# A rarely taken branch's body in the straight line and announced early, and accumulator banks opened with f16 instead of f32 zeros

## The chip, the core and the metric

The kernel runs on one core of one Trainium2 chip. The core has five instruction streams: TensorE (PE; its weight loads are listed apart as PEld), VectorE (DVE), ScalarE (ACT), GpSimd (POOL) and SyncE (SP, which only issues DMAs). The metric is the device time of one execution in microseconds (us), as the median of several executions. A "q" behind an engine's name in a row (PEldq) means the engine's sequencer: waits, branches and issues, during which the engine itself may still work through what was queued.

## What is computed

One decoder layer on 256 tokens of width 2048, all in float32 at the interface. The change touches the second of its three parts, a retrieval of single-neuron experts (PEER). Of 128 x 128 = 16384 experts each token picks 16 in each of 8 heads:

```
eidx, gates = top16 of (key scores a + key scores b), softmax      # per token and head
act  = gelu(u[eidx] . x)                                           # one number per pick
out  = sum over picks of gates * act * v[eidx]                     # 2048 wide
x    = LN2(alpha * x + out)
```

In front of it stand two kinds of attention with LN1; behind it `x = LN3(alpha*x + sigmoid(x W_g) * (p W_p))`.

## The kernel before

The first 88 tokens are treated sparsely: POOL gathers the rows of u and v that they picked (tile `gb`), and DVE multiplies and adds them. The other 168 tokens (`NDT`) are treated densely on TensorE, in two phases:

- The **u phase** multiplies all 128 groups of 128 experts by the 168 tokens, one f32 product of 128 x 128 by 128 x 168 per sixteenth of the width (tile `ps_u`), and ACT takes the gelu (L1114). DVE, ACT and small f16 products (`ps_G`) turn that into a weight per expert and token, which goes to memory (`s_w`), and into a list of the experts that any of these tokens picked.
- The **v phase** walks that list in blocks of 128 experts. For each block POOL gathers two tiles, `vf` (128 rows of v, 1 MB) and `wc` (their weights, 128 x 168); TensorE multiplies each of the 16 column blocks of `vf` by `wc` and adds into six banks of PSUM, `psv` (`v_mm`, L1209). Five buffers of `vf` (`WF`) and eight of `wc` turn around; a gather waits until TensorE has released its buffer.

The list's length is known only at run time. A fixed number of blocks is always done (46 and 40, `CAPS`); 42 further blocks (`rest`) are done only if the list is longer. That is the branch of L1334: `more` is a count that DVE makes, every engine loads it into a register (L1252) and compares it with zero. On TensorE the body of the branch is 672 products. On these inputs the list fits, so the body is jumped over. The instructions of one engine lie in memory in one order: first the code ahead of the compare, then the arms of the branch in an order that `preferred_fallthrough_block` sets, then the code behind. The false arm holds the bookkeeping of the skipped work: on TensorE one wait for its own earlier products with an addition to its counter, on POOL four waits and one addition.

The last three of the always done blocks (`held`) are multiplied behind the branch, bank by bank, so that DVE can add each finished bank to the residual (`v_out`, L1224) while TensorE goes on; then follow transposes (`res2`, L1278 and L1280, with the sparse part's products L915 and L917), LN2, and the gate product `ps_gate` (L217 to L219), whose weights `ple_gate` SP loads and ACT and DVE split in two (L119, L120).

Before the first `v_mm`, each of the six banks is opened by a product of zeros (`v_bank`, L1216), so that all later products can add: the stationary operand is the f32 identity, the moving one a column of zeros read 504 times (three groups of 168; 168 times for the last bank). The first four banks are those that the u phase used, so an opening waits until ACT has taken the gelu out of that bank.

The order of each engine's instructions is made by a scheduler with a simulated timeline; `keep` pins an instruction to the order in which it is written.

Of the kernel before, what the change touches and what calls it, by code (L numbers as in the profile page):

```python
# [9 lines left out]
F32 = mybir.dt.float32  # L10
F32R = mybir.dt.float32r
F16 = mybir.dt.float16
# [7 lines left out]
P = 128  # L20
# [45 lines left out]
STAG, LEAD, NWC = 3, 4, 8  # L66
# [92 lines left out]
def build(tc, a, out):  # L159
    nc = tc.nc  # L160
# [6 lines left out]
    def pbank(pool, name, tag="bank", bufs=4):  # L167
        return pool.tile([P, 512], F32, name=name, tag=tag, bufs=bufs)
# [3 lines left out]
    ident = c0p.tile([P, P], F32, name="ident")  # L172
# [446 lines left out]
    gin = pools.open("gin", "left", bufs=1)  # L619
    io128 = gin.tile([P, P], F16, name="io128")  # L620

    zero = gin.tile([P, 1], F32, name="zero")
    nc.gpsimd.memset(zero, 0.0)
    eig, eact, ew = [], [], []
    for i, (_, n) in enumerate(GROUPS):
# [55 lines left out]
    keep = tc.keep_in_program_order  # L681
# [131 lines left out]
    def gathers(n):  # L813

        nonlocal due
        due += n
        while due >= 1:
            due -= 1
            run(sparse, 1)
# [283 lines left out]
    def run(work, n):  # L1103

        for _ in range(n):
            if next(work, "end") == "end":
                return True
        return False
# [63 lines left out]
    rest = [(i, b) for i, (_, n) in enumerate(PARTS) for b in range(CAPS[i], n)]  # L1172

    def v_fetch(i, b, vpool, wpool, tags):

        vf = vpool.tile([P, D], F32, name="vf", tag=tags[0], bufs=WF if vpool is sup else 1)
        wc = wpool.tile([P, NDT], F32, name="wc", tag=tags[1], bufs=NWC if vpool is sup else 1)
        for dst, src, idx in ((wc, a[f"s_w{i}"].rearrange("p a t -> (p a) t"), idxW[i]),
                              (vf, a["v_rows"], idxV[i])):
            keep(nc.gpsimd.indirect_dma_start(  # L1180
                out=dst, out_offset=None, in_=src,
                in_offset=bass.IndirectOffsetOnAxis(ap=idx[:, b:b + 1], axis=0)))
        return vf, wc
# [24 lines left out]
    def v_mm(d, vf, wc, last):  # L1208
        return nc.tensor.matmul(psv[d // 3][:, d % 3 * NDT:(d % 3 + 1) * NDT],  # L1209
                                vf[:, d * P:(d + 1) * P], wc, start=False,  # L1210
                                stop=last and (d % 3 == 2 or d == ND - 1))

    def v_bank(pool, n):

        ps = pbank(pool, "ps_v")
        keep(nc.tensor.matmul(ps[:, :n], ident, zero.to_broadcast([P, n]),  # L1216
                              start=True, stop=False))
        return ps

# [8 lines left out]
    def v_blocks(n, wpool, between=lambda: None):  # L1228

        for _ in range(n):  # L1230
            while order and len(fetched) <= LEAD and (not order[0][0] or len(idxV) > 1):
                fetched.append(v_fetch(*order.pop(0), sup, wpool, ("wf", "wc")))
            block = fetched.pop(0)
            for d in range(ND):
                v_mm(d, *block, False)
                if d % 8 == 7:
                    between()

    marked = False
    psv = [v_bank(pp, 3 * NDT) for _ in range(4)] + [v_bank(pa, n * NDT) for n in (3, 1)]  # L1240
    done = False

# [5 lines left out]
    for b in range(CAPS[0]):  # L1248
        if b == CAPS[0] - LEAD:
            while not done:  # L1250
                done = run(work, 1)
            more = nc.values_load(total[0:1, 0:1], min_val=0, max_val=NIA * NKEY)  # L1252
# [70 lines left out]
    N1 = CAPS[1]  # L1323
    for b in range(LEAD + 1, N1 - STAG):
        v_blocks(1, wcq)
        gathers(GV)
        if b == N1 - STAG - 1:
            while not run(sparse, 1):
                pass
# [1 line left out]
    natural_parts(ylp)  # L1331

    fbp = pools.open("fbp", "left", bufs=1)
    with tc.If(more > 0, preferred_fallthrough_block=False):  # L1334
        for i, b in rest:
            block = v_fetch(i, b, fbp, fbp, ("vf", "wc_"))
            for d in range(ND):
                v_mm(d, *block, False)
# [57 lines left out]
    def ln2_T(t, d0, nd):  # L1396
        ps = pbank(pp, "ps_x2T")
        for j in range(nd):
            keep(nc.tensor.transpose(ps[:, j * P:(j + 1) * P],  # L1399
                                     x2[t][:, (d0 + j) * P:(d0 + j + 1) * P], ident))  # L1400
        return ps[:, :nd * P].rearrange("p (j n) -> p j n", j=nd)
# [101 lines left out]
    ps = ln2_T(0, 0, 2)  # L1503
# [17 lines left out]
    ps = ln2_T(1, 0, 4)  # L1521
# [8 lines left out]
    ps = ln2_T(1, 4, 4)  # L1530
# [8 lines left out]
    ps = ln2_T(0, 8, 4)  # L1539
# [7 lines left out]
    ps = ln2_T(0, 12, 4)  # L1547
# [4 lines left out]
    for d0, k0, k1 in ((8, 12, 14), (12, 14, 16)):  # L1552
        ps = ln2_T(1, d0, 4)
# [157 lines left out]
```

## Time and profile before

| | us |
|---|---|
| median of 3 timed runs | 1710.34 (1708.72 to 1712.31) |
| the profiled execution, its own time | 1708.22 |
| its span, first to last instruction | 1706.4 |
| TensorE busy | 1682.3 (99% of the span) |
| weight loads busy | 1563.7 (92%) |
| VectorE, ScalarE, GpSimd busy | 1098.9, 556.1, 609.5 |
| mean granted TensorE clock | 0.997 of full speed |

The profile lists, for every group of instructions, how long the engine was busy in it and how long it stood idle before it, with what ended the idle time; "issue" means that nothing which the profile shows was waited for. TensorE's f32 products appear twice, as two records of weight load and product each. A record's duration (306 ns for 128 x 168) is longer than the distance from one start to the next (142 ns), because products overlap in the array; the distance is what a product costs.

### The profile page before, as it was taken

How to read it: one execution, taken by the hardware profiler on the slowest of the kernel's cores; microseconds unless marked ns; L12 is line 12 of the kernel's file. 1: busy time of each engine (PE TensorE's matmuls, PEld its weight loads, DVE VectorE, ACT ScalarE, POOL GpSimd, SP SyncE). 2: the span in 40 equal slices, each digit the busy share in tenths (PEclk: the TensorE clock that was granted, in tenths of full speed). 3: DMA queues.
4: the chain of work that ended last, by engine and by line, in shares of the span. 5: the costliest groups of instructions: out<-in, count | busy, mean ns of one | idle time of the engine just before them, and what ended most of it. 6: DMA issues, size and time to landing. Idle time of an engine off the chain costs nothing. (4 is left out here: it accounts for less than half of the span.)

```text
span 1706.4 us, 29275 instructions
## 1 busy us (share of the span) xinstructions
PE 1682.3 (99%) x11258; PEld 1563.7 (92%) x11258; DVE 1098.9 (64%) x2290; ACT 556.1 (33%) x1396; POOL 609.5 (36%) x624
## 2 busy tenths in 40 slices
PE   9999999999999999999999999999999999998998
PEld 7888888888889999999999999999999999998886
DVE  5565489763589779844467765785776943333676
ACT  5677468753111100010044552005553000001452
POOL 0134023103345422722232322137554787673000
PEclk9999999999999999999999999999999999999999
DMA  7544644483998999999999999979999999997571
GB/s 294 195 155 162 234 160 156 156 323 133 338 419 327 390 421 417 419 420 421 421 415 405 371 384 392 422 293 394 392 383 382 418 412 415 401 396 281 187 269 50
DMA packets 97444, 555.63 MB, mean 326 GB/s; under 512 B 13366, under 2 KB 16966, under 8 KB 41846
## 3 DMA queue, kind: packets, MB, share of 16 engines
q0 software_dynamic: 43056, 285.38, 41.7%
q1 hardware_dynamic: 52086, 264.99, 40.3%
q10 hardware_dynamic: 2160, 3.34, 0.6%
q8 instruction: 92, 1.51, 0.3%
q14 instruction: 50, 0.41, 0.1%
HBM read 536.80 MB, written 17.04 MB: 325 GB/s over the span
## 5 line engine op out<-in xcount | busy, mean ns | idle before, releaser
L210 PE MATMUL ps_u<-XF,wf 128*128 128x168 f32 x3936 | 581.3, 308 | 7.5 <-DMA wf<-peer_u 7.1
L210 PEld LDWEIGHTS ps_u<-XF,wf 128*128 128x128 f32 x3936 | 562.5, 190 | 14.1 <-issue 11.8
L1209 PE MATMUL ps_v<-wc,vf 128*128 128x168 f32 x2752 | 414.8, 309 | 5.5 <-issue 5.5
L1209 PEld LDWEIGHTS ps_v<-wc,vf 128*128 128x128 f32 x2752 | 395.9, 191 | 7.3 <-issue 6.8
L120 DVE TENSOR_TENSOR wl<-wf,wh 128x1024 fp32r<-128x1024 f32 (+1 forms) x199 | 212.7, 1092 | 109.8 <-ACT wh L119 108.2
L854 DVE SCALAR_TENSOR_TENSOR gb<-gb,xq 128x2048 f32<-128x2048 f32 x88 | 203.4, 2316 | 99.0 <-DMA gb<-u_rows,eig 99.0
L864 DVE SCALAR_TENSOR_TENSOR y<-gb,ew,y 128x2048 f32<-128x2048 f32 x78 | 183.0, 2346 | 76.4 <-DMA gb<-v_rows,eig 76.3
L119 ACT CAST wh<-wf 128x1024 fp32r<-128x1024 f32 (+1 forms) x199 | 172.0, 892 | 121.0 <-PE ps_v L219 33.0
L1114 ACT ACTIVATE A<-ps_u 128x168 f32<-128x168 f32 x128 | 39.6, 310 | 459.7 <-PE ps_u L210 456.8
L198 PE MATMUL ps_qk<-X,wh 128*128 128x512 f32 x512 | 185.2, 401 | 0.0
L886 POOL DMA_INDIRECT gb<-u_rows,eig x88 | 94.6, 1075 | 246.6 <-DVE gb L854 151.4
L886 POOL DMA_INDIRECT gb<-v_rows,eig x88 | 104.3, 1185 | 132.6 <-DVE y L864 36.4
L200 PE MATMUL ps_qk<-X,wl 128*128 128x256 f32 x512 | 145.7, 285 | 0.0
L943 ACT ACTIVATE hi<-eq,ghf 128x68 f16<-128x68 f16 (+1 forms) x336 | 113.0, 336 | 87.4 <-DVE eq L937 87.3
L1180 POOL DMA_INDIRECT vf<-v_rows,idxV x86 | 107.2, 1246 | 83.9 <-PE ps_G L958 45.1
L1180 POOL DMA_INDIRECT wc<-s_w,idxW x86 | 102.9, 1197 | 40.4 <-issue 24.9
L198 PEld LDWEIGHTS ps_qk<-X,wh 128*128 128x128 f32 x512 | 96.4, 188 | 21.9 <-issue 1.0
L210 PE MATMUL ps_q<-XF,wf 128*128 128x256 f32 x512 | 113.5, 379 | 0.0
L944 ACT ACTIVATE lo<-eq,glf 128x68 f16<-128x68 f16 (+1 forms) x336 | 112.3, 334 | 0.0
L968 DVE SCALAR_TENSOR_TENSOR A<-ps_G,A 128x18 f32<-128x18 f32 (+2 forms) x168 | 46.9, 308 | 100.4 <-PE ps_G L958 44.0
L210 PEld LDWEIGHTS ps_q<-XF,wf 128*128 128x128 f32 x512 | 95.9, 190 | 12.3
L200 PEld LDWEIGHTS ps_qk<-X,wl 128*128 128x128 f32 x512 | 96.3, 188 | 2.5 <-issue 1.3
(309 smaller groups left out, 2127.2 us busy)
## 6 DMA issues: line engine op xcount, KB each, us to landing
wf<-peer_u SPq DMA_DIRECT2D x123, 1024.0 KB
wf<-w_qk SPq DMA_DIRECT2D x64, 512.0 KB
wf<-w_out SPq DMA_DIRECT2D x32, 512.0 KB
wf<-peer_wq SPq DMA_DIRECT2D x16, 1024.0 KB
wf<-ple_gate SPq DMA_DIRECT2D x16, 1024.0 KB
s_w<-A SPq DMA_DIRECT2D x14, 672.0 KB
wf<-w_v SPq DMA_DIRECT2D x16, 512.0 KB
wf<-w_sv SPq DMA_DIRECT2D x15, 512.0 KB
```

Of the source, the lines that this page charges most:

```text
L119: self.order(nc.scalar.copy(wh, src))
L120: self.order(nc.vector.tensor_tensor(wl, src, wh.bitcast(F32), op=ALU.subtract))
L198: nc.tensor.matmul(ps, wh[:, j * P:(j + 1) * P], xt[:, dt, :], start=dt == 0, stop=False)
L200: nc.tensor.matmul(ps[:, :T], wl[:, j * P:(j + 1) * P], xt[:, dt, :T], start=False, stop=dt == ND - 1)
L210: nc.tensor.matmul(ps[:, :T - t0], wf[:, dt * P:(dt + 1) * P], xt[:, dt, t0:], start=dt == 0, stop=dt == ND - 1)
L854: keep(nc.vector.scalar_tensor_tensor(g, g, 1.0, xq[i], op0=ALU.mult, op1=ALU.mult, accum_out=eact[i][:, j:j + 1]))
L864: keep(nc.vector.scalar_tensor_tensor(ys[i], g, ew[i][:, j:j + 1], ys[i], op0=ALU.mult, op1=ALU.add))
L886: keep(nc.gpsimd.indirect_dma_start(out=g, out_offset=None, in_=a[kind], in_offset=bass.IndirectOffsetOnAxis(ap=eig[i][:, 0, j:j + 1], axi ...
L943: nc.scalar.mul(hi[:, j, :], eq[:, j, :], ghf[:, t])
L944: nc.scalar.mul(lo[:, j, :], eq[:, j, :], glf[:, t])
L1180: keep(nc.gpsimd.indirect_dma_start(out=dst, out_offset=None, in_=src, in_offset=bass.IndirectOffsetOnAxis(ap=idx[:, b:b + 1], axis=0)))
L1209: return nc.tensor.matmul(psv[d // 3][:, d % 3 * NDT:(d % 3 + 1) * NDT], vf[:, d * P:(d + 1) * P], wc, start=False, stop=last and (d % 3 = ...
```

## The change

Three edits, none of which changes a result. The `zero` column is f16 instead of f32, and the openings use `io128` (an f16 table of 0 to 127, there since the top-k stage) as stationary operand in place of the f32 identity: zero times anything finite is zero. The branch is told to lay its true arm, the body, next behind the compare, where the false arm was. And a place is marked in the loop over v's blocks, one block ahead of the branch in the source, for a hint to TensorE alone that this branch is likely taken.

```
-    zero = gin.tile([P, 1], F32, name="zero")
+    zero = gin.tile([P, 1], F16, name="zero")
...
-        keep(nc.tensor.matmul(ps[:, :n], ident, zero.to_broadcast([P, n]),
+        keep(nc.tensor.matmul(ps[:, :n], io128, zero.to_broadcast([P, n]),
                               start=True, stop=False))
...
     for b in range(LEAD + 1, N1 - STAG):
         v_blocks(1, wcq)
         gathers(GV)
+        if b == N1 - STAG - 2:
+
+            tc.mark_branch_hint_location("rest", "LikelyTaken", [mybir.EngineType.PE])
...
-    with tc.If(more > 0, preferred_fallthrough_block=False):
+    with tc.If(more > 0, preferred_fallthrough_block=True, label="rest"):
```

In the built programs the streams of DVE, ACT and SP hold the same instructions in the same order; POOL's differs only in the order of the branch's two arms. On TensorE three places differ.

First, the openings at the start of the v phase (`ps_u` is the u phase's bank, `ps_v` a bank of v, `io_4038` is io128). Before:

```order
L210 MATMUL ps_u<-XF,wf 128x168 x52
L1216 MATMUL ps_v<-zero,ident 128x504 x3
L1209 MATMUL ps_v<-wc,vf 128x168 x7
L1216 MATMUL ps_v<-zero,ident 128x504 x2
L1216 MATMUL ps_v<-zero,ident 128x168
L1209 MATMUL ps_v<-wc,vf 128x168 x9
```

And in the change:

```order
L210 MATMUL ps_u<-XF,wf 128x168 x52
L1216 LDWEIGHTS io_4038
L1216 MATMUL ps_v<-zero,io_4038 128x504
L1216 LDWEIGHTS io_4038
L1216 MATMUL ps_v<-zero,io_4038 128x504
L1216 LDWEIGHTS io_4038
L1216 MATMUL ps_v<-zero,io_4038 128x504
L1209 MATMUL ps_v<-wc,vf 128x168 x9
L1216 LDWEIGHTS io_4038
L1216 MATMUL ps_v<-zero,io_4038 128x504
```

Two more openings and 7 products follow. The openings of banks 4 to 6 moved from behind 7 products to behind 9, and each is one weight load and one product where an f32 product runs as two of both.

Second, the branch on TensorE, before (672 products are 42 blocks; the second 672 is the body, the first the blocks ahead of the branch; TENSOR_LOAD reads the count):

```order
L1209 MATMUL ps_v<-wc,vf 128x168 x672
L1252 TENSOR_LOAD total
L1334 COMPARE_AND_BRANCH
L1334 UNCONDITIONAL_BRANCH
L1209 MATMUL ps_v<-wc,vf 128x168 x672
L1334 UNCONDITIONAL_BRANCH
L1209 MATMUL ps_v<-wc,vf 128x168 x18
```

And in the change:

```order
L1209 MATMUL ps_v<-wc,vf 128x168 x672
L1252 TENSOR_LOAD total
L1337 COMPARE_AND_BRANCH
L1209 MATMUL ps_v<-wc,vf 128x168 x672
L1337 UNCONDITIONAL_BRANCH x2
L1209 MATMUL ps_v<-wc,vf 128x168 x18
```

Before, the false arm lies directly behind the compare and ends in the branch that jumps over the body; now the compare itself jumps over the body, to a false arm that lies directly ahead of the code behind the branch, so that this arm's own closing branch leads to the next instruction.

Third, the hint. TensorE's stream in the change begins:

```order
L1704 UNCONDITIONAL_BRANCH
L1704 BRANCH_PREFETCH_HINT
L319 MATMUL ps_zero<-M 128x256 x3
L217 MATMUL ps_v<-wh,X 128x512 x2
L218 MATMUL ps_v<-wl,X 128x512 x2
```

The hint waits for nothing, nothing pins it, and the scheduler has put it at the very beginning of the program, some 1560 us of work ahead of the branch; it stands nowhere else.

## Rows read from the trace of the kernel before

**Rows 1.** The page: busy time of the engines and their share.
```profile
PE 1682.3 (99%) x11258; PEld 1563.7 (92%) x11258; DVE 1098.9 (64%) x2290; ACT 556.1 (33%) x1396; POOL 609.5 (36%) x624
```

**Rows 2.** Waits of TensorE from 1150 us on: total us, times, longest.
```profile
PE ps_v L1209 <- issue: 5.5, 2, 5.4
PE ps_x2T L1399 <- ACT x L1417: 0.5, 1, 0.5
PE ps_fin L1601 <- ACT diag L1598: 0.5, 1, 0.5
```

**Rows 3.** TensorE's timeline at the openings: start, length, merged records.
```profile
1155.51 2.88 PE L1216 MATMUL ps_v<-zero,ident 128*128 128x504 f32 x6
1158.23 2.16 PE L1209 MATMUL ps_v<-wc,vf 128*128 128x168 f32 x14
1160.22 2.15 PE L1216 MATMUL ps_v<-zero,ident 128*128 128x504 f32 x6
1162.21 2.73 PE L1209 MATMUL ps_v<-wc,vf 128*128 128x168 f32 x18
1164.77 0.19 PE L951 MATMUL ps_G<-hi,ohb 128*128 128x60 f16 x1
1164.80 0.19 PE L952 MATMUL ps_G<-lo,ohb 128*128 128x60 f16 x1
```

**Rows 4.** Weight loads and ScalarE at the openings, from their timelines.
```profile
1157.27 0.30 PEld L1216 LDWEIGHTS ps_v<-zero,ident 128*128 128x128 f32 x2 [0.72 <-ACT A L1114]
1156.93 0.48 ACT L1114 ACTIVATE A<-ps_u 128x168 f32<-128x168 f32 x2
```

**Rows 5.** Instructions that fill `ps_v`, L1216's records: ns min/median/max, first and last start.
```profile
L1216 PE MATMUL ps_v<-zero,ident x12: 305/586/690, 1155.5 to 1162.1; 128*128 128x504 f32 x10, 128*128 128x168 f32 x2
```

**Rows 6.** Waits of GpSimd from 1150 to 1563 us.
```profile
POOL vf L1180 <- PE ps_G L958: 45.1, 27, 2.9
POOL vf L1180 <- PE ps_v L1209: 27.3, 24, 3.0
```

**Rows 7.** TensorE's timeline at the branch.
```profile
1559.83 3.58 PE L1209 MATMUL ps_v<-wc,vf 128*128 128x168 f32 x24
1568.78 4.95 PE L1209 MATMUL ps_v<-wc,vf 128*128 128x168 f32 x17 [5.37 <-issue]
1573.92 2.98 PE L1209 MATMUL ps_v<-wc,vf 128*128 128x168 f32 x19 [0.18 <-issue]
```

**Rows 8.** The branch's line: sequencer records, ns min/median/max, first and last start.
```profile
L1334 POOLq EVENT_SEMAPHORE  x4: 17/43/6210, 1554.4 to 1560.8; - x4
L1334 PEldq COMPARE_BRANCH  x2: 95/2552/5008, 1561.3 to 1563.6; - x2
L1334 PEldq EVENT_SEMAPHORE  x1: 51/51/51, 1563.5 to 1563.5; - x1
```

**Rows 9.** Busy time by stretch: length, engines (records), clock (PEclk), DMA share, GB/s.
```profile
1100.00:1104.00 4.00, 2.74 (x19) 2.77 (x20) 4.00 (x24) 0.00 (x0) 1.34 (x3) 1.00 1.02 426
1563.40:1568.70 5.30, 0.02 (x1) 0.00 (x0) 2.50 (x4) 2.18 (x4) 0.00 (x0) 0.80 0.70 209
1568.80:1573.90 5.10, 4.93 (x17) 4.65 (x17) 0.00 (x0) 0.00 (x0) 0.00 (x0) 0.54 0.49 199
1574.00:1579.00 5.00, 5.00 (x36) 5.00 (x37) 1.70 (x3) 0.37 (x1) 0.00 (x0) 1.00 0.02 3
```

**Rows 10.** Code queue q8, packets, MB, share: 0 to 1563.4 us, then 1563.5 to 1574.
```profile
q8 instruction: 84, 1.38, 0.3%
...
q8 instruction: 2, 0.03, 1.1%
```

**Rows 11.** The other engines behind the branch, from the timeline.
```profile
1564.22 2.18 ACT L119 CAST wh<-wf 128x512 fp32r<-128x512 f32 x4 [6.74 <-DMA wf<-ple_gate]
1564.87 2.50 DVE L120 TENSOR_TENSOR wl<-wf,wh 128x512 fp32r<-128x512 f32 x4 [6.18 <-ACT wh L119]
1574.36 0.68 DVE L1224 SCALAR_TENSOR_TENSOR XF<-XF,ps_v 128x504 f32<-128x504 f32 x1 [7.00 <-PE ps_v L1209]
```

## The prediction

> **What bounds the kernel now.** The page comes first: TensorE is busy for 99% of the span [rows 1]. A share over the whole does not say what one stretch is worth, so next I read TensorE's waits from the start of the v phase to the end [rows 2]. One line stands out, 5.5 us before v's products, put to "issue"; no other wait there exceeds 0.5 us. From 1150 us on TensorE is the bound with nothing behind it, and a microsecond taken out of its stream should come off the span until something else is late. The change touches two places of that stream.
>
> At the openings [rows 3] the first group (banks 1 to 3) starts at 1155.51 and the first v product at 1158.23; the second group takes from 1160.22 to 1162.21. Six openings leave twelve records [rows 5]. A second view shows what the first hides: the weight load of the third opening waits 0.72 us, until 1157.27, for ScalarE's gelu [rows 4]. ScalarE takes its last two banks only at 1156.93, so TensorE's slow openings are mostly a way of waiting.
>
> At the branch [rows 7] TensorE's work ends at 1559.83 + 3.58 = 1563.41, and goes on at 1568.78 after 5.37 us. [...] At full clock 18 records take 1164.77 - 1162.21 = 2.56 us [rows 3], 0.142 each, 17 of them 2.42. So the branch costs 1573.92 - 1563.41 - 2.42 = 8.1 us. The branch's own records say why [rows 8]: a compare at 1561.3 (95 ns), a wait that ends with TensorE's last product at 1563.5, and then a branch of 5008 ns. Two packets of code of 16 KB each fall into that stretch [rows 10]: one for the target, one for what follows.
>
> **The change, part by part.** *Openings.* One f16 pass goes by the small f16 products: 60 columns are 0.027 us apart [rows 3], so 504 columns are 0.22 us and 168 are 0.07. The first two openings shrink to 0.44 us, but the third still waits until 1157.27, since ScalarE's order and inputs are the same. The first v product then starts at 1157.27 + 0.22 = 1157.49, a gain of 0.74. The fourth opening needs the bank whose gelu ends at 1156.93 + 0.48 = 1157.41, long past. The second group falls from 1.99 us to 2 x 0.22 + 0.07 = 0.51, a gain of 1.48. Together 2.2 us, of twelve records that looked like 4.7. Were an f16 pass of 504 columns as slow as one f32 record (0.42: four of these and two short ones fill the second group's 1.99), it would be 0.54 + 1.0 = 1.5. The upper end is 2.4. What supplies the v phase follows TensorE: the gathers of `vf` waited 27.3 and 45.1 us for products to release buffers [rows 6], and no line of waits has TensorE behind them [rows 2]. I take no loss there; the lower end is 1.0.
>
> *Branch, the order of its arms.* Before, the jump stood behind the false arm's wait, so the fetch began only when TensorE was dry, although its sequencer was at the compare 2.1 us earlier. Now the compare jumps and the wait comes after it. Even unannounced, the 5.0 us begin at 1561.3, on the scale of before.
>
> *Branch, announced.* If the hint brings the target in ahead, the compare costs what a compare that stays costs now, 95 ns [rows 8], and TensorE stops only for the false arm's wait and restart: from 1563.41 to about 1563.8, 0.4 us (0.2 to 0.8).
>
> *The next piece of code.* Before, 17 records after the target came the second gap: the second packet, 5.2 us (1573.92 - 1568.7) after the first piece was entered. The openings lose 12 entries and the hint adds one, so edges between pieces stand 11 entries later, and 22 to 23 records fit behind the target: 3.2 us at full clock. If the second piece is asked for when the jump is decided (1561.4 to 1563.4), it is there at 1566.6 to 1568.6; TensorE runs dry at 1563.8 + 3.2 = 1567.0. The stall is 0 to 1.6, and I take 0.8.
>
> [...] So the branch costs 0.4 + 0.8 = 1.2 us in place of 8.1, a gain of 6.9 (5.7 to 7.9).
>
> *What is queued elsewhere.* The hint is one entry at a moment when TensorE waits for its first data: nothing. GpSimd now jumps over the body's 84 gathers at its compare, but its false arm waits 6210 ns for earlier gathers anyway [rows 8]; that covers a fetch as long as TensorE's, and without this cover it would cost up to 5 us on POOL, which nobody waits for here. Next late after TensorE is VectorE: it must finish four splits (1564.87 + 2.50 = 1567.37 [rows 11]) before the first `v_out`, 0.68 us, which TensorE's first transposes need. These stand 36 products' records behind the branch: 1563.8 + 5.1 + 0.8 = 1569.7, against 1568.05. The cover is 1.7 us, and if the load of `ple_gate` behind the splits does not come 2.2 us earlier too, it is short by 0.5. I take 0 and keep 0.6 for the range.
>
> The sum: 2.2 + 6.9 = 9.1 us. Against the profiled execution, 1708.22 - 9.1 = 1699.1; the median of the timed runs is 2.1 us above that execution, so 1701.2.
>
> **Rivals.** *One: the hint is without effect from where it stands.* The source marks a place one block ahead, but the built order has it as TensorE's first entry, 1560 us early, and no row of this trace shows a hint, let alone one that lasts so long. Against this rival: nothing else on TensorE is hinted or branches in between, and the hint carries its branch, not a time. Then the compare takes 5.0 us from 1561.3, TensorE resumes at 1566.4 after 3.0 us, and the second piece arrives at 1566.4 + 5.2 = 1571.6, against 3.2 us of work (6.4 at half clock, since it is open whether the clock falls). Lost: 5.0 or 6.2 instead of 8.1, so 1.9 to 3.1 gained, 4.1 to 5.3 with the openings: about 1705.6. [...]
>
> *Two: the branch gains nothing.* The compare could be held until TensorE is dry, or the clock falls again and the second piece comes late. Then only the openings stay: 1710.3 - 2.2 = 1708.1. For it speaks that 17 records at half clock now hide the second fetch; against it, that the compare at 1561.3 ran ahead of 2.1 us of queued products.
>
> [...]
>
> **How the numbers follow.** Forecast 0.64, rival one 0.20, two 0.10, three 0.06. About 0.2%, 3.4 us, is what a measurement of this kernel can tell from no change. The forecast is faster by that; of rival one I count 0.16 as faster and 0.04 as within it; rival two is within it; three is slower. So faster 0.80, same 0.14, slower 0.06. The range must reach over rival one, to 1706.5; downward, 2.4 + 7.9 = 10.3 gives 1700.0, and with a microsecond for the spread of medians 1699.0.
>
> **What would show it.** Right: openings with six records instead of twelve, the third still behind L1114, the first v product 0.7 us nearer to the u phase's end; at the branch one jump near 0.1 us on TensorE, idle under 1 us, a second gap under 2 us about 22 records later, and a clock of 1.00 throughout. [...] If the openings' gain is given back as waits for `vf` in the first v blocks, or VectorE's `v_out` ends TensorE's wait before the transposes, my last-but-one paragraph of the parts was wrong.

## The result and the profile after

The changed kernel takes 1700.76 us (median of 4 runs, 1697.44 to 1701.25) against 1710.76 us (1708.72 to 1712.31) for the kernel before: a ratio of 0.9938, interval 0.9921 to 0.9955, 10.0 us less. The forecast was 1701.2. The profiled execution took 1701.25 us, its span is 1698.6. Between the two profiles the spans differ by 7.8 us; the section on the prediction says where the other two are.

TensorE's waits from 1150 us on (total us, times, longest) answer to [rows 2]:

```profile
PE ps_v L1216 <- ACT A L1114: 1.0, 1, 1.0
PE ps_u L210 <- DMA wf<-peer_u: 0.5, 1, 0.5
PE ps_x2T L1402 <- ACT x L1420: 0.5, 1, 0.5
PE ps_fin L1604 <- ACT diag L1601: 0.5, 1, 0.5
PE ps_v L1209 <- PEq L1337: 0.4, 1, 0.4
```

The 5.5 us put to "issue" are gone. In their place stand 0.4 us that end with TensorE's own sequencer at the branch (L1337 is L1334 of before). A new line stands on top: an opening that waits 1.0 us for ScalarE's gelu. What was hidden in TensorE's slow zeros as a wait of the weight load [rows 4] is now open.

The openings, from TensorE's timeline (start, length, merged records), beside [rows 3]:

```profile
1157.53 0.59 PE L1216 MATMUL ps_v<-zero,io 128*128 128x504 f16 x2
1159.10 0.37 PE L1216 MATMUL ps_v<-zero,io 128*128 128x504 f16 x1 [0.98 <-ACT A L1114]
1159.31 2.73 PE L1209 MATMUL ps_v<-wc,vf 128*128 128x168 f32 x18
1161.87 0.66 PE L1216 MATMUL ps_v<-zero,io 128*128 128x504 f16 x3
1162.38 2.19 PE L1209 MATMUL ps_v<-wc,vf 128*128 128x168 f32 x14
```

Six records in place of twelve [rows 5]. From the first opening to the first v product it is 1159.31 - 1157.53 = 1.78 us, where it was 2.72, and half of it is the wait for ScalarE. The second group takes 1162.38 - 1161.87 = 0.51 us, where it was 1.99.

The branch, from TensorE's timeline, the branch's sequencer records (ns min/median/max, first and last start) and the busy time by stretch (the last three figures are the granted clock, the DMA share and GB/s), beside [rows 7 to 9]:

```profile
1563.69 5.37 PE L1209 MATMUL ps_v<-wc,vf 128*128 128x168 f32 x36 [0.36 <-PEq L1337]
1568.89 0.38 PE L1280 MATMUL ps_y<-ident,XF 128*128 128x128 f32 x2
```
```profile
L1337 PEldq COMPARE_BRANCH  x1: 962/962/962, 1561.2 to 1561.2; - x1
L1337 PEldq EVENT_SEMAPHORE  x1: 51/51/51, 1563.4 to 1563.4; - x1
```
```profile
1563.00:1564.00 1.00, 0.64 (x5) 0.42 (x4) 0.00 (x0) 0.00 (x0) 0.00 (x0) 1.00 0.12 41
1564.00:1569.00 5.00, 5.00 (x37) 5.00 (x36) 3.09 (x5) 2.18 (x4) 0.00 (x0) 1.00 0.74 233
```

The one jump takes 962 ns and is over at 1562.2, before the products that were queued ahead of it are done; the wait behind it ends at 1563.4 with the last of them, and TensorE goes on after 0.36 us. All 36 products' records that stand ahead of the transposes follow without a second gap, and the clock stays at 1.00, where it was 0.80 and 0.54.

The code queue of the kernel after (packets, MB, share), from the start to 1562 us, then from 1562 to 1574:

```profile
q8 instruction: 84, 1.38, 0.3%
...
q8 instruction: 2, 0.03, 1.0%
```

These are the counts of [rows 10]: no packet was added. Before, the jump took 5.0 us although a packet had come 1.5 us ahead of the compare; after, a packet comes 1.4 us ahead of it, and the jump takes 0.96 us. The next two packets start at 1566.2 and 1571.7 us before, 2.6 and 2.2 us ahead of the points where TensorE goes on (1568.78 and 1573.92 [rows 7]), and at 1563.1 and 1567.6 after. No view names what a packet holds, so which of them the jump waits for is not shown.

### The profile page after: what moved, and what is told of

The parts are those of the page before. It is cut to its first block, busy times and chain, and to the rows that moved or that the text cites. A ratio compares the mean times of both kernels' runs of the same rounds, so it can differ in the third digit from the quotient of the medians.

```text
span 1698.6 us, 29259 instructions
## 1 busy us (share of the span) xinstructions
PE 1677.5 (99%) x11252; PEld 1560.3 (92%) x11252; DVE 1098.8 (65%) x2290; ACT 556.1 (33%) x1396; POOL 602.5 (35%) x624
## 5 line engine op out<-in xcount | busy, mean ns | idle before, releaser
L1180 POOL DMA_INDIRECT vf<-v_rows,idxV x86 | 103.8, 1207 | 86.2 <-PE ps_G L958 37.6
L1180 POOL DMA_INDIRECT wc<-s_w,idxW x86 | 99.3, 1155 | 40.5 <-issue 24.6
```

What stands on the lines that cost most here:

```text
L1180: keep(nc.gpsimd.indirect_dma_start(out=dst, out_offset=None, in_=src, in_offset=bass.IndirectOffsetOnAxis(ap=idx[:, b:b + 1], axis=0)))
```

## The experiments

They came in three sets, each with runs of the kernel before on the same chip: the edits alone and the two of the branch together (first four), the changed kernel with its neighbours (next four), and the last four. The kernel before itself took 1715.82, 1716.33 and 1710.4 us in these sets; in the first two, profiles show stops in the first v blocks that the profiles of the last set and the first profiles of before and after do not have (below), so times there carry a disturbance that comes without any edit, though it need not be equally large with each. The first and the third set ran on one chip and the second on another, so the chip alone does not explain it. That is why I read two stages of each profile beside the times: from the first opening to the last `ps_G` product (150 us later, the openings' and first v blocks' stage), and from there to the first `ps_y` transpose (the branch's stage). Both are differences of starts in TensorE's timeline.

| kernel | ratio to before, 95% interval | opening to last `ps_G`, us | last `ps_G` to first `ps_y`, us |
|---|---|---|---|
| before | | 153.22 | 268.00 |
| after | 0.9938 (0.9921 to 0.9955) | 150.84 | 260.53 |
| openings alone | 1.001 (0.9995 to 1.0024) | 163.43 | 267.73 |
| arm order alone | 0.9967 (0.9954 to 0.9981) | 160.44 | 264.23 |
| hint alone, old order | 0.9984 (0.9969 to 0.9999) | 161.77 | 267.29 |
| order and hint | 0.9955 (0.9937 to 0.9973) | 159.66 | 260.19 |
| before, second set | | 158.11 | 268.36 |
| after, second set | 0.9966 (0.9954 to 0.9979) | 159.64 | 260.20 |
| late openings | 0.9973 (0.9962 to 0.9984) | 156.41 | 260.24 |
| 226 instructions more | 1.0031 (1.002 to 1.0042) | 168.13 | 262.29 |
| after, third set | 0.9937 (0.9924 to 0.9951) | 150.98 | 261.17 |
| order and hint, third set | 0.9952 (0.9937 to 0.9967) | 153.23 | 260.26 |
| 28 instructions more | 0.9934 (0.992 to 0.9947) | 150.89 | 260.52 |
| zeros behind the branch | 0.9964 (0.9947 to 0.9981) | 150.95 | 261.49 |

### Openings alone

```
-    zero = gin.tile([P, 1], F32, name="zero")
+    zero = gin.tile([P, 1], F16, name="zero")
...
-        keep(nc.tensor.matmul(ps[:, :n], ident, zero.to_broadcast([P, n]),
+        keep(nc.tensor.matmul(ps[:, :n], io128, zero.to_broadcast([P, n]),
```

> Only the six openings are changed (f16 zeros on io128); the branch is as before. My theory: the first group is cut short only to the point where ScalarE's gelu ends, the third opening waits about 1 us for L1114, the second group falls from 1.99 to about 0.5 us; 2.2 to 2.4 us in all, ratio 0.9986; the branch costs 8 us as before. Rival, that all twelve records count: 3.4 us or more, no wait of the third opening. Rival, that the gain is given back in the v phase: ratio 1.000 and new waits of TensorE for vf.

No gain was measured. The openings themselves did what was expected: the third waits 1.13 us for ScalarE and the second group takes 0.51 us. The gain went a few microseconds later. TensorE's timeline from the second block on, and the busy time from 1160 to 1200 us:

```profile
1166.39 0.25 PE L958 MATMUL ps_G<-eq,ohb 128*128 128x60 f16 x3 [0.50 <-issue]
1168.52 1.28 PE L1209 MATMUL ps_v<-wc,vf 128*128 128x168 f32 x4 [1.66 <-issue]
1170.66 1.15 PE L1209 MATMUL ps_v<-wc,vf 128*128 128x168 f32 x3 [0.86 <-issue]
1173.49 1.84 PE L1209 MATMUL ps_v<-wc,vf 128*128 128x168 f32 x6 [1.68 <-issue]
```
```profile
1160.00:1200.00 40.00, 35.30 (x294) 33.84 (x293) 20.11 (x42) 13.27 (x54) 22.32 (x22) 0.87 0.97 376
```

Stops of 4.7 us in these rows, none put to another engine or to a DMA. The clock fell as well: its mean is 0.87 over these 40 us, and 1.00 in the profiles without stops, which is up to 5.2 us of work lost (an estimate, 0.13 of 40). With 7.4 us of idle time put to "issue" ahead of the branch, that comes to the 12.6 us by which this first stage is longer than the changed kernel's (163.43 against 150.84). Whether the edit brings them or the execution could not be said from this run; the next sets were made for that.

### Arm order alone

```
-    with tc.If(more > 0, preferred_fallthrough_block=False):
+    with tc.If(more > 0, preferred_fallthrough_block=True, label="rest"):
```

> Only the order of the branch's arms is changed; no hint, openings as before. My theory: the far jump is now the compare, about 5 us from about 2 us before TensorE is dry, so TensorE is idle about 3 us in place of 5.4; the next piece of code comes late or the clock falls; 1.9 to 3.1 us faster in all, ratio 0.9985. Rival, that the order alone is what helped: idle under 1 us, 6 us or more faster. Rival, that the compare waits until TensorE is dry: idle 5 us, ratio 1.000.

Better than expected: 4.0 us in the branch's stage (268.2, the mean of the two profiles of before, less 264.2), 5.7 us (3.3 to 7.9) by the times. The branch's records, TensorE's timeline and the busy time behind the jump:

```profile
L1334 PEldq COMPARE_BRANCH  x1: 4337/4337/4337, 1573.3 to 1573.3; - x1
```
```profile
1577.99 2.66 PE L1209 MATMUL ps_v<-wc,vf 128*128 128x168 f32 x17 [2.54 <-PEq L1334]
1582.04 2.98 PE L1209 MATMUL ps_v<-wc,vf 128*128 128x168 f32 x19 [1.39 <-issue]
```
```profile
1578.00:1582.00 4.00, 2.65 (x17) 2.40 (x17) 1.67 (x3) 0.70 (x2) 0.00 (x0) 1.00 0.67 233
```

This is rival one as described, the unannounced jump that begins while TensorE still works, but cheaper: 4.3 us and not 5.0, a second gap of 1.39 us and not 2.0, and the 17 records behind it run at full speed (2.66 us; 4.95 in [rows 7]). After 2.54 us of idle time the clock was 1.00 from 1578 to 1582 us; after 4.25 and 5.28 us (next run and the one before) it was 0.50 there.

### Hint alone

```
+        if b == N1 - STAG - 2:
+            tc.mark_branch_hint_location("rest", "LikelyTaken", [mybir.EngineType.PE])
...
-    with tc.If(more > 0, preferred_fallthrough_block=False):
+    with tc.If(more > 0, preferred_fallthrough_block=False, label="rest"):
```

> Only the hint is added; the false arm lies next to the compare as before, and the far jump is that arm's own branch, which no hint names. My theory: the hint speaks of the compare alone, so the 5008 ns branch stays, idle about 5.4 us, ratio 1.000. Rival, that the hint loads whatever lies behind the branch: idle under 1 us, 6 us or more faster. If a standing hint disturbs the fetching of the program, this run shows it as well: slower.

```profile
L1336 PEldq COMPARE_BRANCH  x2: 104/1998/3892, 1572.0 to 1574.3; - x2
```
```profile
1578.33 4.82 PE L1209 MATMUL ps_v<-wc,vf 128*128 128x168 f32 x16 [4.25 <-issue]
```
```profile
1578.00:1582.00 4.00, 3.67 (x13) 3.71 (x14) 0.00 (x0) 0.00 (x0) 0.00 (x0) 0.50 0.80 293
```

The far jump is still the false arm's closing branch, still begun when TensorE is dry, and takes 3892 ns; the clock falls as before (0.50). The branch's stage gains 0.9 us, about what the jump is shorter than the 5.0 us of before; the ratio's interval ends at 0.9999. So a hint on a compare that isn't the far jump gave little.

### Order and hint

The two edits above together.

> The order of the arms and the hint, openings as before. My theory: all that the branch gives, 6.9 to 8 us, ratio 0.9955; compare 0.1 to 1.5 us, TensorE idle about 0.4 us, no fall of the clock. Rival, that the two parts of the change help one another: less than the change's 10 us by more than the openings' 2.4. The start of the program, where the changed kernel's profile was 1.2 us later than the one before, is late here too if the hint causes it, and not if it is chance.

```profile
L1336 PEldq COMPARE_BRANCH  x1: 662/662/662, 1569.6 to 1569.6; - x1
```

TensorE idles 0.30 us, and 36 records follow without a gap. Beside the arm order alone the hint is worth 264.23 - 260.19 = 4.0 us; the two together 8.0, where each alone gives 4.0 and 0.9. It is the stage that shows this: by the times the two ratios, 0.9967 and 0.9955, have intervals that overlap.

### The kernel before and the changed kernel in the second set

> The kernel before, unchanged, profiled once more beside the next three. The profiles of the four single edits showed idle time of TensorE put to issue in the first v blocks (1160 to 1320 us, 12.2 us in the openings-only kernel), which the first profiles of before and after do not have. If this idle time comes with the execution and not with an edit, this profile has it too, several us between the openings and 1320; if it comes from an edit, this profile has less than 0.5 us there. At the branch: compare about 0.1 us, jump about 5.0 us, TensorE idle 5.3 us.

> The changed kernel, unchanged, once more, as the yardstick for the next two. My theory (openings 2.4 us, branch 7.9 us, nothing given back): ratio 0.994, compare about 1 us, idle at the branch 0.4 us. Rival, from the openings-only kernel, which gained nothing: the openings' gain is given back in the first v blocks; then 0.9953, and idle time put to issue between the openings and 1320 us that is longer than in the kernel before by about 2 us.

The kernel before shows the stops too, so they come without any edit: 0.43 us at 1172.43, 0.52 at 1193.16, and 3.4 in all beside those of the branch. The changed kernel has 4.5. In its timeline, most of them begin among the small f16 products (`ps_G`) of the second batch:

```profile
1169.67 0.19 PE L958 MATMUL ps_G<-eq,ohb 128*128 128x60 f16 x1 [0.54 <-issue]
1170.35 0.22 PE L958 MATMUL ps_G<-eq,ohb 128*128 128x60 f16 x2 [0.50 <-issue]
1171.05 0.41 PE L1209 MATMUL ps_v<-wc,vf 128*128 128x168 f32 x1 [0.48 <-issue]
1171.76 0.44 PE L1209 MATMUL ps_v<-wc,vf 128*128 128x168 f32 x1 [0.30 <-issue]
1173.17 1.00 PE L1209 MATMUL ps_v<-wc,vf 128*128 128x168 f32 x3 [0.96 <-issue]
```

The starts are 0.70 us apart, or twice that, and one or a few instructions come with each. So here the ratio is 0.9966: the branch's stage keeps its 8.2 us, the first stage loses 1.5 instead of gaining 2.4.

The stops alone, 1.1 us longer than in the kernel before, do not make these 3.9 us. The clock can account for most of it. The busy time of the changed kernel from 1170 to 1180 us, where the clock of the kernel before is 1.00:

```profile
1170.00:1180.00 10.00, 7.18 (x38) 6.17 (x39) 4.62 (x10) 1.87 (x8) 4.07 (x4) 0.66 1.02 419
```

At a mean of 0.66 up to 3.4 us of work are lost (an estimate, 0.34 of 10). From 1160 to 1200 us the clock's mean is 0.83 to 0.96 in all four profiles of these two sets with f16 openings; of the four with f32 openings it is 0.91 in one (hint alone) and 1.00 in three. Whether the f16 openings help the fall along is not shown by so few executions.

GpSimd is slower in the same profiles. Its gathers of `vf` between 1200 and 1300 us (busy us, mean ns of one, idle before), in the first profile of before and in that of the second set:

```profile
L1180 POOL DMA_INDIRECT vf<-v_rows,idxV x19 | 18.4, 970 | 37.0 <-PE ps_G L958 37.0
```
```profile
L1180 POOL DMA_INDIRECT vf<-v_rows,idxV x19 | 28.0, 1471 | 12.5 <-PE ps_G L958 9.1 <-issue 3.0 <-PE ps_G L952 0.3
```

The mean is 1362 to 1490 ns in the eight profiles of the first two sets and 970 to 1051 in the other six. So what disturbs these executions is not TensorE's alone; which of the two follows the other is not shown.

### Late openings

```
-                v_mm(d, *block, False)
+                if d % 3 == 0 and len(psv) == d // 3:
+                    psv.append(v_bank(pp, 3 * NDT) if d < 12 else v_bank(pa, min(3, ND - d) * NDT))
+                (keep if d < 12 and len(psv) < 6 else lambda i: i)(v_mm(d, *block, False))
...
-    psv = [v_bank(pp, 3 * NDT) for _ in range(4)] + [v_bank(pa, n * NDT) for n in (3, 1)]
+    psv = []
```

> The changed kernel with each bank opened only ahead of its own first product, so that three v products stand between one opening and the next; nothing else is moved except that the first 16 v products and the openings between them keep their written order. Theory: the wait of the third opening for ScalarE's last gelu (0.98 us after the change) is filled with six products of 0.14 us, so it shrinks to 0.1 to 0.4 us and the time by 0.6 to 0.9 us, ratio to the kernel before 0.0004 below the changed kernel's. Rival: the v phase is limited in its first blocks by something other than TensorE's stream (the idle time put to issue); then the products start earlier, the idle time grows by as much, and the end does not move.

The wait for ScalarE is gone: the third opening starts 2.14 us after the first, with twelve records in between, and waits for nothing.

```profile
1156.73 0.38 PE L1216 MATMUL ps_v<-zero,io 128*128 128x504 f16 x1
1156.94 1.02 PE L1209 MATMUL ps_v<-wc,vf 128*128 128x168 f32 x6
1157.80 0.38 PE L1216 MATMUL ps_v<-zero,io 128*128 128x504 f16 x1
1158.01 1.02 PE L1209 MATMUL ps_v<-wc,vf 128*128 128x168 f32 x6
1158.87 0.38 PE L1216 MATMUL ps_v<-zero,io 128*128 128x504 f16 x1
```

The time (1710.91 us, against 1711.14 for the changed kernel beside it) does not show it; the stops in this set are larger than the 1.0 us. Without them it was not tried.

### 226 instructions more ahead of the branch

```
+    pads = [113]
+
     def v_bank(pool, n):
...
         keep(nc.tensor.matmul(ps[:, :n], io128, zero.to_broadcast([P, n]),
                               start=True, stop=False))
+        if pads:
+            for _ in range(pads.pop()):
+                keep(nc.tensor.matmul(ps[:, :2], io128, zero.to_broadcast([P, 2]),
+                                      start=False, stop=False))
```

> The changed kernel with 113 more products of zeros of two columns in the first opening (226 more instructions with their weight loads, about 3 us of TensorE), so that everything behind lies 226 instructions later in TensorE's code. Theory: a hint works whatever the place of the branch in its code piece: compare 0.1 to 1 us, idle at the branch 0.3 to 0.5 us, time above the changed kernel by the 3 us of the added products alone. [...]

The theory fell. The branch's record, TensorE's timeline behind it, and the code queue from 1579.9 to 1584.5 us (in the 14 us ahead of that it has no packet):

```profile
L1343 PEldq COMPARE_BRANCH  x1: 4192/4192/4192, 1579.9 to 1579.9; - x1
```
```profile
1584.40 5.37 PE L1209 MATMUL ps_v<-wc,vf 128*128 128x168 f32 x36 [2.40 <-PEq L1343]
```
```profile
q8 instruction: 1, 0.02, 1.3%
```

In the changed kernel a packet stands between 1559.5 and the compare at 1561.2; here the compare comes first and takes 4.2 us, near the 4.3 us of the jump without a hint, and TensorE idles 2.40 us. So with the hint in place the jump was long once; what decides it stays open (see the run with 28 instructions).

The added products cost far more than their 3 us. TensorE's timeline and the busy time from 1164 to 1168 us:

```profile
1159.39 1.30 PE L1222 MATMUL ps_v<-zero,io 128*128 128x2 f16 x43
1161.17 0.23 PE L1222 MATMUL ps_v<-zero,io 128*128 128x2 f16 x3 [0.47 <-issue]
1161.90 0.28 PE L1222 MATMUL ps_v<-zero,io 128*128 128x2 f16 x5 [0.50 <-issue]
1162.62 0.24 PE L1222 MATMUL ps_v<-zero,io 128*128 128x2 f16 x4 [0.45 <-issue]
...
1171.19 1.10 PE L1222 MATMUL ps_v<-zero,io 128*128 128x2 f16 x36 [0.48 <-issue]
```
```profile
1164.00:1168.00 4.00, 1.25 (x14) 0.61 (x14) 0.00 (x0) 0.00 (x0) 3.23 (x5) 0.50 0.98 372
```

43 follow each other in 1.3 us, then groups of one to five come every 0.72 us, and after 10 us the last 36 pass in 1.1 us. These products wait for no other engine and no DMA; what holds them up no row names. The clock is at 0.50 from 1164 to 1176 us, and that is part of the cost; the steps are not of the clock, since they begin at 1161.17, and the clock's mean is still 0.94 from 1160 to 1164.

### The changed kernel, and order and hint, in the third set

> The changed kernel once more, beside the next run, which differs from it by the openings alone. [...]

> Arm order and hint, f32 openings left: the branch's gain of 7.9 us without the openings' 2.4. Theory (both gains add up): ratio 0.0014 above the changed kernel's. Rival (the openings' gain is given back in the first v blocks): the same ratio as the changed kernel's, within 0.0006.

No stop is left in these two profiles, and the gains add up. The changed kernel takes 1700.37 us, the one with f32 openings 1703.41: 3.0 us, by the first stage 2.25. The two ratios differ by 0.0015, as the theory said; their intervals overlap, so it is the stage that shows it.

One new line stands in the changed kernel's timeline behind the branch:

```profile
1570.15 0.44 PE L1280 MATMUL ps_y<-ident,XF 128*128 128x128 f32 x2 [0.65 <-DVE XF L1224]
```

TensorE waits for VectorE's `v_out`. VectorE's splits of `ple_gate` began at 1567.00 here (1564.83 in the first profile of after, at nearly the same point of the program), since ScalarE's, ahead of them, waited 8.65 us for the load instead of 6.76.

### 28 instructions more

The same edit as above with `pads = [14]`.

> The changed kernel with 14 products of zeros of two columns added in the first opening: 28 instructions more ahead of everything that follows, 0.4 us of TensorE. [...] Time: the changed kernel's plus 0.4 us.

The compare takes 937 ns, so 28 instructions more leave the jump as short as in the changed kernel: it takes 0.6 to 1.2 us in all the profiles with hint and new order except that of the 226 instructions. The first v blocks show no stop. The zeros cost nothing: they fill the wait for ScalarE (0.68 us left of 1.13).

### The 113 products of zeros behind the branch

```
             for i, block in enumerate(held):
                 keep(v_mm(d, *block, i == STAG - 1))
+        if bank == 2:
+            for _ in range(113):
+                keep(nc.tensor.matmul(psv[5][:, :2], io128, zero.to_broadcast([P, 2]),
+                                      start=False, stop=False))
```

> The changed kernel with the 113 products of zeros of the run with 226 added instructions, but behind the branch, after the ninth product of the third bank, where the DMA engines are half as busy (200 to 220 GB/s against 400 at the openings). [...] Rival (a supply of some 7 instructions per us is the limit everywhere): stops of 0.45 to 0.55 us between groups of 1 to 5 products as at the openings, 10 us or more for the stretch, and the time 10 us above.

```profile
1571.49 3.01 PE L1369 MATMUL ps_v<-zero,io 128*128 128x2 f16 x113
1574.36 0.88 PE L1280 MATMUL ps_y<-ident,XF 128*128 128x128 f32 x3
```
```profile
1574.00:1578.00 4.00, 4.00 (x38) 3.82 (x36) 1.05 (x3) 0.59 (x1) 0.00 (x0) 0.60 0.01 4
```

All 113 in 3.01 us, 0.027 each, without one stop; the time is 4.65 us above the changed kernel's, and most of the rest lies right behind them, where the granted clock is 0.60 from 1574 to 1578 us. So short instructions as such are not limited to the 7 per us of that run (34 products with their weight loads in 10 us). Whether the gathers or the set makes the difference stays open: this set has no stops at the openings either, and GpSimd, which issues the gathers, is idle here.

## Why the prediction was right, and where it was off

**Openings**: forecast 2.2, measured 0.94 + 1.48 = 2.4 us in the profile of after, and 2.4 by the stage (153.22 - 150.84). The step that carried it is that the weight load's hidden wait sets the first group; the f16 price was 0.22 us per pass as taken (1159.31 - 1159.10 = 0.21 behind the third opening). Had the two groups' whole 4.7 us been taken to shrink to six passes (1.2 us), the forecast would have been 3.5.

**Branch**: forecast 6.9; by the idle time 8.1 - 0.36 = 7.7, by the stage 268.00 - 260.53 = 7.5. Two sizes were off. The compare takes 962 ns, not the 95 of a compare that stays; it costs nothing, since the wait behind it ends 1.2 us later, but the cover is that small. And the second gap, priced at 0.8 between 0 and 1.6, is not there. No run shows that term: in all nine profiles with hint and new order TensorE passes the 36 records behind the jump without a gap. The 0.8 and its 22 to 23 records were an estimate from the 17 records and the 5.2 us of the kernel before; where one piece of code ends and when the next is asked for, no view shows. Behind the jump one packet falls between 1561.2 and 1566 and one between 1566 and 1574, and neither stops TensorE. The step that failed is that the 5.2 us of before were carried over to the new order.

**The hint's place**: rival one (it is without effect from 1560 us ahead) is refuted by the pair with and without hint: 662 against 4337 ns. Where nothing is announced, the far jump took 4337 to 5008 ns in four profiles, and with the hint and 226 instructions more ahead of the compare, where no packet came in the 14 us before it, 4192; in the other eight profiles with hint and new order it took 602 to 1187. Why it is short in these and long in that one is not shown. That it might be long with the hint in place was no rival of mine, and would have cost 2.1 us (262.29 - 260.20 in the branch's stage).

**Rival two, and the chance of slower**: the clock stayed at 1.00 behind the branch, and TensorE's waits hold no line put to "issue".

**VectorE's cover**: taken as 0 with 0.6 kept for the range. It held in the first profile of after, and was short by 0.65 and 1.03 us in two others, for the reason given there: the load of `ple_gate` does not come earlier with TensorE.

**The total**: the profiled execution of after is 7.0 us shorter than that of before, not 9.1. By the stages 2.4 + 7.5 = 9.9 us were gained; the u phase ended 2.0 us later in it (1157.39 against 1155.37), and 0.8 us more lay around the span. Whether the 2.0 us are the change's is not shown. The u phase ends at 1155.4 to 1155.8 us in three of the four profiles without the hint, but at 1160.0 in the fourth (arm order alone), and at 1156.1 to 1159.0 in the ten with it. The medians, 10.0 us apart here and in the third set, agree with the stages alone, which speaks for chance. That the forecast of 1701.2 lies within 0.5 us of the measured median is luck in part: the gain was forecast 0.9 us too small, but the kernel before stood at 1710.34 then and at 1710.76 in the final measurement, which hid half of it.

**Not foreseen**: "what supplies the v phase follows TensorE" held for data. In two of three sets something else did not follow in the first v blocks, and the openings' gain was lost there, to the stops and, in the kernels with f16 openings, to a clock that fell among them. What makes the stops stays open. Shown is that they befall the kernel before too, that they part instructions that wait for nobody, in steps of 0.7 us, that GpSimd's gathers are slower in the same executions (1362 to 1490 ns against 970 to 1051), and that all of this can be absent altogether.

## What to carry to other kernels

Here a jump over a rarely run body cost about what it stuck out from behind queued work (4.3 us, begun 2.1 us before TensorE was dry, left 2.54 us idle): put the far jump on the compare, ahead of the wait (4.0 us here), and then announce it (4.0 more); the hint on the old layout gave 0.9. Look at the jump's own sequencer record after every edit ahead of it: with the hint in place it took 4192 ns behind 226 more instructions, 937 behind 28. And price a step that hides a wait by the wait's end, not by the step's records: six halved openings gave 2.4 us and left a 1 us wait that later openings or other work can fill.

## What was not expected of the hardware

- A hinted, taken far compare took 602 to 1187 ns in eight of nine profiles, a compare that stays 95 to 104, a far jump that no hint names 3892 to 5008.
- A hint that stands 1560 us ahead was still of use (662 ns with it, 4337 without), but with 226 instructions more ahead of the branch the compare came before any packet and took 4192 ns.
- After an idle time of 2.54 us at the branch the clock was 1.00, after 4.25, 5.28 and 5.37 us about 0.5. It fell with TensorE busy too: behind the 113 two-column products it was 0.60 from 1574 to 1578 us, with no idle time from 1570 on.
- Starts of TensorE's instructions 0.70 to 0.72 us apart over up to 10 us, with nothing waited for, in two sets of runs and not in the others. In the profiles of these two sets a gather of `vf` between 1200 and 1300 us took GpSimd 1362 to 1490 ns on average, in the others 970 to 1051.
